# Three attention stages in another order, and latent queries in six column tiles

## The chip, the cores and the metric

The kernel runs on one core of a Trainium2 chip. The metric is device time in microseconds (us) of one launch, from runs without the profiler; one further execution was recorded by the hardware profiler, and all rows below come from it. Five engines work side by side and meet at semaphores: TensorE (PE, matrix products; PEld is its weight load), VectorE (DVE), ScalarE (ACT, with function tables), GpSimd (POOL) and SyncE (SP, which here only issues DMAs).

## The reference

256 tokens of width 1024 go through two layers of a first block and one of a second, all in float32:

```python
for l in range(DEPTH):                                   # first block, 2 layers
    a = hybrid_mixer(rms_norm(x, pre_mix_g[l]), ...)     # latent + dilated attention
    x = x + rms_norm(a, post_mix_g[l])
    c = memory_cross_attention(rms_norm(x, pre_xattn_g[l]), rms_norm(mem, mem_g[l]), ...)
    x = x + rms_norm(c, post_xattn_g[l])
    hdn = jnp.square(jax.nn.relu(rms_norm(x, pre_mlp_g[l]) @ w_up[l]))
    x = x + rms_norm(hdn @ w_down[l], post_mlp_g[l])
# second block, 1 layer
u, v, q, kv, gl = jnp.split(h @ w_in[l], splits, axis=-1)
a = spatial_gating_unit(gelu(u), gelu(v), ...)           # 128 x 128 causal mixing of tokens
b = nsa_attention(q, kv, gl, ...)                        # compressed, selected and window branches
x = x + concat(rms_norm(a, ...), rms_norm(b, ...)) @ w_out[l]
x = x + memory_cross_attention_2(...)
x = x + square(relu(h @ w_ff1[l])) @ w_ff2[l]
```

The latent queries, which the change rebuilds, are, with 8 heads of 64 plain ("nope") and 32 rotated ("rope") columns and a scale of 96 ** -0.5 in the scores:

```python
q = (rms_norm(c_q, q_norm_g) @ w_uq).reshape(B, S, 8, 96)
q = concat([q[..., :64], rope(q[..., 64:], positions)], axis=-1)
```

rope(x) is [x1 * cos - x2 * sin, x2 * cos + x1 * sin] of the two halves of 16. The compressed branch of nsa_attention joins 32 tokens to one block, sends it through gelu(flat @ w1 + b1) @ w2 + b2 and scores 15 such keys per query.

## The kernel before, in words

Every product of activations with weights is made of float32r parts. A weight chunk of 128 rows is loaded by DMA into a staging buffer (raw, 4 buffers; load_w, L164), ACT writes its rounded high part (L170, or L174 with the norm's gain), DVE the rest (L171, L175) into one of 8 whl buffers. A product is then three matmuls (mm3, L182 to L184): high by high, high by low, low by high. Activations have the same two parts in hT, oT, mem or mid, here as [2, kt, T]: all high parts of the kt chunks, then all low parts.

Three helpers run the projections over k, the chunks of 128 of the inner dimension. projA takes tokens as the PE's weights and moves 512 weight columns. projB takes weight columns as PE's weights and moves 256 tokens, by mm3 into two halves of a bank. projS does the same with two matmuls: L248 moves 512 values, the high and low tokens of chunk k, which lie 8 KB apart, and L249 moves 256. Each takes a table `at`: at[k] names a function that is called ahead of chunk k, so transposes of one stage can be put between matmuls of another. PSUM has 4 banks with the name ps, 2 with tp, and one each of pf0 and pf1.

A scheduler sets each engine's order from the order in which the code is written and from priorities: V, A and G (DVE, ACT and POOL) go through the class Ahead, whose operations count as 600 places earlier; weights use nc.vector and nc.scalar, without that. All operations through Ahead carry L135 in the profile, so there one goes by tile names.

The stages that the change touches, in order of time:

- the start: 12 small matmuls warm PE up (L469), then x is normalised and transposed. Query and key/value latents are transposed into cT by transp_split (L278) from k=2 and k=5 of the first projS; rows() (L628) transposes the rotary tables; then come key rotations (krs) and a second projS, and memory([0]) and memory([1]) transpose mem.
- latent(), once per layer: w_uq is split as 8 heads of 96 columns, L752 and L753 copy its rope columns swapped behind them (128 per head), four projB calls make q in 8 tiles of two heads, all in bank pf1, and DVE evacuates each with a multiplication by the table Mq into qT. Keys and values follow. L436 makes scores from kT and qT, L405 transposes the exponentials e, and L446 multiplies the transposes eT by the values.
- mem_attention: scores (L851) and values (L859) of two halves of 128 tokens; turn() transposes a half's queries and copies them to qT. cross2 (the second block) uses it too, with qn transposed at L1390.
- mlp: up01 makes the first two of eight column blocks; turn() transposes relu results (L902), called at k=3 of a later projection.
- mixer2: the gated part (u, v), then keys, hidden (the compressed MLP's first layer, L1083, weights cmp_w1 straight from raw), queries, and a table MIX2 that says which piece runs beside which attention group. mk and mv are projections of the second block's memory; cscores (L1273) scores the 15 compressed keys; gates() takes Exp, strips() Gelu, which lie in different function tables of ACT.

## Time and profile before

| | |
|---|---|
| Runs | 1208.45, 1209.34, 1210.66 us (median 1209.34) |
| Profiled execution | 1207.37 us |
| Span of its instructions | 1205.3 us |
| PE busy | 1178.3 us (98%) |
| PE weight loads | 981.8 us (81%) |
| DVE busy | 810.4 us (67%) |
| ACT busy | 716.5 us (59%) |
| POOL busy | 83.6 us (7%) |
| DMA | 213.12 MB, mean 177 GB/s |

The span begins with the first instruction and ends with the last; the execution holds 2.07 us more around it. A matmul counts as busy from its start to its modelled end, and the next starts before that end; so what a matmul costs in a stream is read from starts, not from its duration. "Idle before" is the time in which an engine did nothing ahead of an instruction, and the releaser is the instruction whose semaphore came last. Tile names leave buffer numbers out.

### The profile page before, as it was taken

How to read it: one execution, taken by the hardware profiler on the slowest of the kernel's cores; microseconds unless marked ns; L12 is line 12 of the kernel's file. 1: busy time of each engine (PE TensorE's matmuls, PEld its weight loads, DVE VectorE, ACT ScalarE, POOL GpSimd, SP SyncE). 2: the span in 40 equal slices, each digit the busy share in tenths (PEclk: the TensorE clock that was granted, in tenths of full speed). 3: DMA queues.
4: the chain of work that ended last, by engine and by line, in shares of the span. 5: the costliest groups of instructions: out<-in, count | busy, mean ns of one | idle time of the engine just before them, and what ended most of it. 6: DMA issues, size and time to landing. Idle time of an engine off the chain costs nothing.

```text
span 1205.3 us, 17865 instructions
## 1 busy us (share of the span) xinstructions
PE 1178.3 (98%) x6430; PEld 981.8 (81%) x6430; DVE 810.4 (67%) x1583; ACT 716.5 (59%) x1492; POOL 83.6 (7%) x161
## 2 busy tenths in 40 slices
PE   8999999999999999999999999999999999999998
PEld 6788888888888898778888788887877787888887
DVE  6777766576676676766757676667658657766653
ACT  7766655565565575755648565557676557655551
...
GB/s 263 296 183 223 98 216 196 59 233 194 191 180 197 116 265 196 148 190 157 208 90 193 240 179 200 195 178 166 198 207 106 88 88 138 211 191 188 183 192 35
DMA packets 92182, 213.12 MB, mean 177 GB/s; under 512 B 7285, under 2 KB 21055, under 8 KB 91327
## 3 DMA queue, kind: packets, MB, share of 16 engines
...
## 4 chain that ended last, share of the span: by engine, by line
PE 76%; DMA 7%; DVE 7%; ACT 6%; issue 2%; POOL 1%; SPq 0%; ACTq 0%; POOLq 0%; DVEq 0%
PE ps L184 11%; PE ps L182 11%; PE ps L183 11%; PE pf L248 8%; PE tp L248 6%; PE pf L249 4%; PE pf L182 4%; PE pf L184 4%; PE pf L183 4%; DVE whl L175 3%; PE tp L249 3%; ACT whl L174 2%; DMA raw<-in_w_in_dram 2%; PE ps L446 2%; PE ps L851 1%
## 5 line engine op out<-in xcount | busy, mean ns | idle before, releaser
L175 DVE SCALAR_TENSOR_TENSOR whl<-raw,gT,whl 128x512 fp32r<-128x512 f32 (+5 forms) x416 | 295.0, 750 | 99.1 <-ACT whl L174 98.7
L174 ACT ACTIVATE whl<-raw,gT 128x512 fp32r<-128x512 f32 (+5 forms) x416 | 277.0, 717 | 131.0 <-issue 59.8
L171 DVE TENSOR_TENSOR whl<-raw,whl 128x512 fp32r<-128x512 f32 x264 | 170.3, 686 | 79.6 <-ACT whl L170 79.1
L170 ACT ACTIVATE whl<-raw 128x512 fp32r<-128x512 f32 x264 | 153.7, 628 | 110.7 <-issue 77.7
L182 PE MATMUL ps<-whl,mid 128*128 128x512 f32 x384 | 150.5, 392 | 0.0
L184 PE MATMUL ps<-whl,mid 128*128 128x512 f32 x384 | 149.8, 390 | 0.0
L183 PE MATMUL ps<-whl,mid 128*128 128x512 f32 x384 | 149.6, 390 | 0.0
L248 PE MATMUL pf<-hT,whl 128*128 128x512 f32 x352 | 132.6, 399 | 0.0
L248 PE MATMUL tp<-hT,whl 128*128 128x512 f32 x288 | 107.9, 398 | 0.0
L249 PE MATMUL pf<-hT,whl 128*128 128x256 f32 x352 | 98.8, 281 | 0.0
L182 PE MATMUL ps<-whl,hT 128*128 128x512 f32 (+4 forms) x240 | 85.6, 356 | 0.0
L184 PEld LDWEIGHTS ps<-whl,mid 128*128 128x128 f32 x384 | 72.1, 188 | 15.6
L184 PE MATMUL ps<-whl,hT 128*128 128x512 f32 (+4 forms) x240 | 84.1, 350 | 0.4 <-DVE hT L135 0.4
L182 PEld LDWEIGHTS ps<-whl,mid 128*128 128x128 f32 x384 | 72.1, 188 | 15.1
L183 PE MATMUL ps<-whl,hT 128*128 128x512 f32 (+4 forms) x240 | 84.1, 350 | 0.0
L183 PEld LDWEIGHTS ps<-whl,mid 128*128 128x128 f32 x384 | 72.1, 188 | 14.5
L249 PE MATMUL tp<-hT,whl 128*128 128x256 f32 x288 | 80.9, 281 | 0.0
L248 PEld LDWEIGHTS pf<-hT,whl 128*128 128x128 f32 x352 | 66.1, 188 | 16.2 <-DVE qkd L135 0.3
L249 PEld LDWEIGHTS pf<-hT,whl 128*128 128x128 f32 x352 | 66.5, 189 | 0.0
L248 PEld LDWEIGHTS tp<-hT,whl 128*128 128x128 f32 x288 | 54.1, 188 | 13.2 <-DVE mem L135 0.2
L182 PE MATMUL ps<-whl,oT 128*128 128x512 f32 x152 | 60.8, 400 | 0.0
L184 PE MATMUL ps<-whl,oT 128*128 128x512 f32 x152 | 59.7, 393 | 0.0
...
## 6 DMA issues: line engine op xcount, KB each, us to landing
...
```

The lines of the kernel that those rows point to most:

```text
L170: nc.scalar.activation(hl[:, 0, c:d], raw[:, c:d], AF.Copy)
L171: nc.vector.tensor_tensor(out=hl[:, 1, c:d], in0=raw[:, c:d], in1=hl[:, 0, c:d].bitcast(F32), op=ALU.subtract)
L174: nc.scalar.activation(hi[:, i], r[:, i], AF.Copy, scale=g[i])
L175: nc.vector.scalar_tensor_tensor(lo[:, i], r[:, i], g[i], hi[:, i].bitcast(F32), ALU.mult, ALU.subtract)
L182: PE.matmul(o, sh, mh, start=start, stop=False, skip_group_check=True)
L183: PE.matmul(o, sh, ml, start=False, stop=False, skip_group_check=True)
L184: PE.matmul(o, sl, mh, start=False, stop=stop, skip_group_check=True)
L248: PE.matmul(banks[c], hi[:, cs], xT[2][:, :, k], start=k == 0, stop=False, skip_group_check=True)
L249: PE.matmul(banks[c][:, 0], lo[:, cs], xT[0][:, k], start=False, stop=k == KT - 1, skip_group_check=True)
L446: PE.matmul(cell["o"][j * 64:j * 64 + 64, h // 2], vf(h, kb), pp[j][i][kb] if bias is None else pp[j][i][kb][:, ::-1], start=begin and i = ...
L851: PE.matmul(s[:, i], qT[:, c, tq], kT[:, c], start=(i == 0 and k == 0), stop=k == nkt - 1, skip_group_check=True)
```

## The change

- latent() splits w_uq into 256 rope columns of all heads and 512 nope columns, without swapped copies. Three tiles of two times 128 columns are made, in banks pf1, pf0, pf1. The rope tile is copied by ACT to SBUF and multiplied by csq, once for cos (DVE) and once for sin (POOL), for each of four pairs of heads; the nope tiles are scaled by ACT while copied. The sum of the two products for rotation is taken over by the keys: krs holds them a second time with halves swapped.
- hT, oT and mem become [kt, 2, T]: high and low part of a chunk side by side.
- 15 warm-up matmuls. Transposes at k=1 and 6; rows() at k=2 and memory at k=5 and 7 of the second projS; krs behind it.
- turn1() ahead of values(0) in mem_attention; in cross2 the squares of the queries come from the copy qn, behind the qT copy, and the weights of the last mlp (ff1) are held until that copy.
- up01's turn at k=5, down's at n=6, mixer2's first at k=6.
- The first half of cmp_w1 is loaded ahead into a large tile (w1; oT takes its tile later), hidden(0) is spread over four places of the next projection; gates() waits for the last Gelu; ckeys and cscores stand earlier, two banks in turn.

```diff
-MIX2 = {1: "gating ckeys0 mk0 ckeys", 2: "mk1 norm0", 3: "norm1 first0 cprobs", 4: "finish0 mkn first1 rn0", 5: "mv0",
+MIX2 = {1: "gating mk0", 2: "mk1 norm0", 3: "norm1 first0 cprobs", 4: "finish0 mkn first1 rn0", 5: "mv0",
         6: "out0"}
 
 IDENT, TRI, CM, VALID, BLK, ROPE, ONES, SEL, NCOL = 0, 128, 256, 286, 288, 296, 300, 301, 331
...
-                PE.matmul(banks[c], hi[:, cs], xT[2][:, :, k], start=k == 0, stop=False, skip_group_check=True)
+                PE.matmul(banks[c], hi[:, cs], xT[2][:, k], start=k == 0, stop=False, skip_group_check=True)
...
-        h = h16p.tile([128, 2, kt, T], F32R, tag="h16", name=nm)
-        return (h[:, 0], h[:, 1], h)
+        h = h16p.tile([128, kt, 2, T], F32R, tag="h16", name=nm)
+        return (h[:, :, 0], h[:, :, 1], h)
...
-    for _ in range(12):
+    for _ in range(15):
         PE.matmul(b, warm, warm.unsqueeze(1).to_broadcast([128, 16, 32]), start=True, stop=True)
...
-        V.tensor_scalar(Mq, M, 96.0 ** -0.5, None, ALU.mult)
-        V.memset(Mq[0:64], 96.0 ** -0.5)
+        for g in range(4):
+            nc.vector.tensor_scalar(csq[32 * g:32 * g + 32, 0], M[64:96], 96.0 ** -0.5, None, ALU.mult)
+            nc.scalar.activation(csq[32 * g:32 * g + 32, 1], M[96:128], AF.Copy, scale=-(96.0 ** -0.5))
...
-                                    at={2 + 3 * t: lambda t=t: transp_split(cns[t], t, cT, 0, 5) for t in range(2)})):
+                                    at={1 + 5 * t: lambda t=t: transp_split(cns[t], t, cT, 0, 5) for t in range(2)})):
...
-            rows()
             memory = load_mem(I["mem"])
+        wd = load_all(w, 8, 1184, 512, gp)
+        for i, b in enumerate(projS(wd, hT, 4, ["ps", "ps", "pf0", "pf1"], at={2: rows, 5: lambda: memory([0]), 7: lambda: memory([1])} if l == 0 else {})):
+            halves(qkd[:, 1, i], b)
...
-                hl = whlp.tile([128, 2, 8, 128], F32R, tag="whl", name="whl")
+                hl = whlp.tile([128, 2, 768], F32R, tag="whl", name="whl")
                 g = GI["q_norm_g", l][k]
-                nc.scalar.activation(hl[:, 0, :, 0:96], raw, AF.Copy, scale=g)
-                nc.vector.scalar_tensor_tensor(hl[:, 1, :, 0:96], raw, g, hl[:, 0, :, 0:96].bitcast(F32), ALU.mult, ALU.subtract)
-                for i in range(2):
-                    f32v = hl[:, i].bitcast(F32)
-                    nc.vector.tensor_copy(hl[:, i, :, 96:112], f32v[:, :, 80:96])
-                    nc.vector.tensor_copy(hl[:, i, :, 112:128], f32v[:, :, 64:80])
-                wq.append((hl[:, 0].rearrange("p h c -> p (h c)"), hl[:, 1].rearrange("p h c -> p (h c)")))
+                for c0, n, o in ((64, 32, 0), (0, 64, 256)):
+                    hi, lo = (hl[:, i, o:o + 8 * n].rearrange("p (h c) -> p h c", h=8) for i in range(2))
+                    nc.scalar.activation(hi, raw[:, :, c0:c0 + n], AF.Copy, scale=g)
+                    nc.vector.scalar_tensor_tensor(lo, raw[:, :, c0:c0 + n], g, hi.bitcast(F32), ALU.mult, ALU.subtract)
...
-            for i in range(4):
-                b, = projB([(h_[:, i * 256:], l_[:, i * 256:]) for h_, l_ in wq], cT, 2, "pf1")
-                V.tensor_tensor(out=qT[:, 2 * i:2 * i + 2], in0=b, in1=Mq.unsqueeze(1).to_broadcast([128, 2, T]),
-                                op=ALU.mult)
+            for i in range(3):
+                b = ps([128, 2, 256], f"pf{(i + 1) % 2}")
+                for k, (h_, l_) in enumerate(wq):
+                    for c in range(2):
+                        cs = slice((2 * i + c) * 128, (2 * i + c) * 128 + 128)
+                        mm3(b[:, c], h_[:, cs], l_[:, cs], cT[0][:, k], cT[1][:, k], k == 0 and c == 0, k == 2)
+                if i == 0:
+                    rope = sc([128, 2, T])
+                    A.activation(rope, b, AF.Copy)
+                    for g in range(4):
+                        pr = slice(32 * g, 32 * g + 32)
+                        for j, eng in enumerate((V, G)):
+                            eng.tensor_tensor(out=qT[64 + 32 * j:96 + 32 * j, g:8:4], in0=rope[pr],
+                                              in1=csq[pr, j].unsqueeze(1).to_broadcast([32, 2, T]), op=ALU.mult)
+                else:
+                    h = 4 * (i - 1)
+                    for j in range(2):
+                        A.activation(qT[0:64, h + j:h + 4:2], b[64 * j:64 * j + 64], AF.Copy, scale=96.0 ** -0.5)
             for i in range(2):
                 b, = projB([(w_[0][0][:, i * 256:], w_[0][1][:, i * 256:]) for w_ in wkv], cT, 2, "pf1", k0=3)
...
+        turn1()
         values(0)
-        turn1()
...
-            ws = [load_all(w_up, 8, j * 512, 512, g) for j in range(2)]
+            if held[0] is None:
+                ws = [load_all(w_up, 8, j * 512, 512, g) for j in range(2)]
+            else:
+
+                with tc.issue_after(held[0].ins):
...
-                    at = {} if turn is None else {3: turn}
+                    at = {} if turn is None else {5: turn}
...
-            last = down(j, mids, {} if j else {3: turn})
+            last = down(j, mids, {} if j else {6: turn})
...
-            uvb = [projA(wuv[i], hT, t, [(0, 512)], at={4: first} if i == 1 and t == 0 else {})[0] for i in range(2)]
+            uvb = [projA(wuv[i], hT, t, [(0, 512)], at={6: first} if i == 1 and t == 0 else {})[0] for i in range(2)]
...
+        w1 = h16p.tile([128, 16, 256], F32, tag="h16", name="w1")
+        for q4 in range(4):
+            nc.sync.dma_start(w1[:, q4 * 4:q4 * 4 + 4],
+                              I["cmp_w1_2"][0, 0, q4 * 512:q4 * 512 + 512, :].rearrange("(m p) n -> p m n", p=128))
...
+            wib[t], = projA(ww, hT, t, [(0, 280)], at={2 * q + 1: lambda q=q: hidden(0, [q]) for q in range(4)} if t else {})
             keys(t)
-            if t == 0:
-                hidden(0)
+        oT = new_hT("oT")
...
+            with tc.issue_after(cell["gelu"].ins):
+                for t in range(2):
+                    A.activation(gate[:, t].rearrange("p h b -> p (h b)"), wib[t][:, 256:280], AF.Exp, scale=-1.0)
...
-        queries(1, projA(wq, hT, 1, [(0, 512)], "pf0", at={0: lambda: hidden(1, [2]), 2: lambda: hidden(1, [3]),
+        queries(1, projA(wq, hT, 1, [(0, 512)], "pf0", at={0: lambda: hidden(1, [2]), 1: ckeys, 2: lambda: hidden(1, [3]),
                                                            3: lambda: keysT(1), 4: lambda: queriesT(0),
-                                                           5: lambda: (strips(1), gates()), 6: gateT})[0])
+                                                           5: lambda: (strips(1), gates()), 6: gateT, 7: ckeysT})[0])
...
-            return {2 * t + h + 1: lambda t=t, h=h: some(t, h) for t in range(2) for h in range(2)}
+            return {2 * t + h + 2: lambda t=t, h=h: some(t, h) for t in range(2) for h in range(2)}
...
-               "first0": lambda: first_half(0), "first1": lambda: first_half(1), "ckeys0": ckeys0, "ckeys": ckeys,
-               "cprobs": cprobs, "finish0": lambda: cell.update(rn=finish(0)), "rn0": lambda: cell["rn"](), "mk0": lambda: mk(0), "mk1": lambda: mk(1, cscores()), "mkn": mkn,
+               "first0": lambda: first_half(0), "first1": lambda: first_half(1),
+               "cprobs": cprobs, "finish0": lambda: cell.update(rn=finish(0)), "rn0": lambda: cell["rn"](), "mk0": lambda: mk(0, cscores()), "mk1": lambda: mk(1, {1: cvalues}), "mkn": mkn,
...
-            ms = head_ms(qb, 4, 128)
-            G.tensor_tensor(out=ms[:, :4], in0=ms[:, :4], in1=r2[t][:, 1:2].to_broadcast([128, 4]), op=ALU.mult)
-            rq[t] = lv()
-            rsqrt_eps(ms[:, :4], 4, r=rq[t])
-            G.tensor_tensor(out=rq[t][:, :4], in0=rq[t][:, :4], in1=r2[t][:, 0:1].to_broadcast([128, 4]), op=ALU.mult)
-
...
-                copy_any(qT[:, :, t * 128:t * 128 + 128], bt)
+                held[0] = copy_any(qT[:, :, t * 128:t * 128 + 128], bt)
+
+                ms = head_ms(qn, 4, 128)
```

PE in cross2, between the last query projection of the second half and the output projection (L405, in the changed file L404, transposes e; L859, there L872, is eT by values; L1390, there L1414, transposes the queries; L851, there L864, makes scores). Before:

```order
L184 MATMUL pf_9443<-whl,hT 128x512
L405 MATMUL tp<-cm,e 128x128 x8
L859 MATMUL ps<-eT,kv_8921 128x128 x8
L1390 MATMUL tp<-cm,sc 128x128 x4
L851 MATMUL ps<-kv_8921,qT 128x256 x4
L182 MATMUL ps<-whl,oT 128x512
```

And of the change:

```order
L183 MATMUL pf_9421<-whl,hT 128x512
L1414 MATMUL tp<-cm,sc 128x128 x2
L404 MATMUL tp<-cm,e 128x128 x3
L1414 MATMUL tp<-cm,sc 128x128 x2
L404 MATMUL tp<-cm,e 128x128 x3
L872 MATMUL ps<-eT,kv_8899 128x128 x4
L404 MATMUL tp<-cm,e 128x128 x2
L872 MATMUL ps<-eT,kv_8899 128x128 x4
L864 MATMUL ps<-kv_8899,qT 128x256 x4
L181 MATMUL ps<-whl,oT 128x512
```

The transposes of the queries moved ahead of the value products, and they and those of e alternate. Next, ACT in mixer2, up to the exponentials of the first window scores (hc is the Gelu, small the gates, kq and vw queries and values, whl the weights of w_out). Before:

```order
L135 ACTIVATE sc<-pf_8360 128x256
L174 ACTIVATE whl<-raw,gT_99 128x1024 x2
L135 ACTIVATE scf<-pf_8360 128x512
L174 ACTIVATE whl<-raw,gT_99 128x1024
L135 ACT_TABLE_LOAD
L135 ACTIVATE e,den<-ps,sm,small 128x128 x8
L135 ACTIVATE junk,sm<-uv 128x512 x2
```

And of the change:

```order
L135 ACTIVATE hc<-hp,gT_99 128x30 x2
L135 ACT_TABLE_LOAD
L135 ACTIVATE small<-ps 128x24 x2
L135 ACTIVATE vw<-tp 128x512
L135 ACTIVATE nx<-tp,gqk 128x30
L173 ACTIVATE whl<-raw,gT_99 128x512
L135 ACTIVATE sc<-pf_8339 128x256
L173 ACTIVATE whl<-raw,gT_99 128x512
L173 ACTIVATE whl<-raw,gT_99 128x1024
L135 ACTIVATE scf<-pf_8339 128x512
L173 ACTIVATE whl<-raw,gT_99 128x1024 x2
L135 ACTIVATE e,den<-ps,sm,small 128x128 x8
L135 ACTIVATE junk,sm<-uv 128x512
```

The function table is loaded once behind the last Gelu, ahead of the gates, and one weight split more comes behind the exponentials. Last, DVE where layer 1's latent query weights are split (raw to whl). Before:

```order
L749 SCALAR_TENSOR_TENSOR whl<-raw,gT_98,whl 128x8x96
L752 CAST whl<-whl 128x8x16
L753 CAST whl<-whl 128x8x16
L752 CAST whl<-whl 128x8x16
L753 CAST whl<-whl 128x8x16
L749 SCALAR_TENSOR_TENSOR whl<-raw,gT_98,whl 128x8x96
L135 TENSOR_TENSOR scf<-pf_4768,scf 128x256
L752 CAST whl<-whl 128x8x16
L753 CAST whl<-whl 128x8x16
L752 CAST whl<-whl 128x8x16
L753 CAST whl<-whl 128x8x16
L749 SCALAR_TENSOR_TENSOR whl<-raw,gT_98,whl 128x8x96
```

And of the change:

```order
L752 SCALAR_TENSOR_TENSOR whl<-raw,gT_98,whl 128x256
L752 SCALAR_TENSOR_TENSOR whl<-raw,gT_98,whl 128x512
L752 SCALAR_TENSOR_TENSOR whl<-raw,gT_98,whl 128x256
L752 SCALAR_TENSOR_TENSOR whl<-raw,gT_98,whl 128x512
L135 TENSOR_TENSOR scf<-pf_4764,scf 128x256
L752 SCALAR_TENSOR_TENSOR whl<-raw,gT_98,whl 128x256
L752 SCALAR_TENSOR_TENSOR whl<-raw,gT_98,whl 128x512
L762 SCALAR_TENSOR_TENSOR whl<-raw,gT_98,whl 128x512 x4
```

Three splits of 8x96 with four casts each became six splits, of 256 and 512 columns, without casts.

## Rows read from the trace of the kernel before

**Rows 1.** The page: the span, and busy us of TensorE (PE).
```profile
span 1205.3 us, 17865 instructions
...
PE 1178.3 (98%) x6430; PEld 981.8 (81%) x6430; DVE 810.4 (67%) x1583; ACT 716.5 (59%) x1492; POOL 83.6 (7%) x161
```

**Rows 2.** View of PE's waits: us in total, times, longest us.
```profile
PE ps L446 <- DVE eT L135: 2.2, 2, 1.8
PE tp L902 <- DVE relu L135: 2.1, 4, 1.1
...
PE ps L859 <- ACT eT L135: 1.8, 3, 1.3
PE tp L405 <- DVE e L135: 1.7, 2, 1.6
PE tp L628 <- DVE cT L135: 1.4, 1, 1.4
PE pf L1083 <- DMA raw<-in_cmp_w_dram: 1.3, 1, 1.3
PE tp L278 <- DVE cT L135: 1.2, 1, 1.2
```

**Rows 3.** Timeline, PE, 838-844 us: start, us, operation, count, idle before.
```profile
838.39 0.85 PE L278 MATMUL tp<-cm,sc 128*128 128x128 f32 x6 [0.55 <-DVE sc L135]
...
843.04 0.50 PE L184 MATMUL ps<-whl,hT 128*128 128x512 f32 x1 [0.39 <-DVE hT L135]
```

**Rows 4.** Groups by shape, PE: operation, count, busy us, mean ns, idle before.
```profile
L182 PE MATMUL ps<-whl,mid 128*128 128x512 f32 x384 | 150.5, 392 | 0.0
...
L248 PE MATMUL pf<-hT,whl 128*128 128x512 f32 x352 | 132.6, 399 | 0.0
...
L182 PE MATMUL pf<-whl,mem 128*128 128x512 f32 x88 | 36.2, 411 | 0.2 <-ACT scf L135 0.2
...
L469 PE MATMUL pf<-mhalf 128*32 128x512 bf16 x12 | 4.8, 581 | 1.0 <-POOL mhalf L135 1.0
```

**Rows 5.** Timeline, PE, layer 0's latent queries.
```profile
116.09 0.28 PE L182 MATMUL pf<-cT,whl 128*128 128x256 f32 x1
...
117.76 0.28 PE L184 MATMUL pf<-cT,whl 128*128 128x256 f32 x1
```

**Rows 6.** Groups by shape, POOL.
```profile
L135 POOL COPY nx<-hc 128x60 f32<-128x60 f32 x4 | 1.1, 324 | 2.5 <-ACT hc L135 2.5
L135 POOL TENSOR_SCALAR_AFFINE_SELECT scf<-scf 128x1024 f32<-128x1024 f32 x1 | 1.1, 1106 | 94.9 <-DMA scf<-in_sg_w_dram 94.9
```

**Rows 7.** Timeline, PE, layer 1's latents.
```profile
518.75 1.09 PE L446 MATMUL ps<-eT,VV 128*64 128x128 f32 x16 [1.82 <-DVE eT L135]
```

**Rows 8.** Timeline, PE, cross2 and the start of its mlp.
```profile
1004.46 1.78 PE L851 MATMUL ps<-kv,qT 128*128 128x256 f32 x7 [1.30 <-ACT qT L135]
...
1021.00 0.39 PE L182 MATMUL pf<-whl,hT 128*128 128x512 f32 x1
...
1023.72 0.39 PE L182 MATMUL pf<-whl,hT 128*128 128x512 f32 x1
```

**Rows 9.** Timeline, ACT, mixer2.
```profile
899.76 1.28 ACT L135 ACT_TABLE_LOAD   x1
```

**Rows 10.** Timeline, PE, mixer2.
```profile
893.45 1.16 PE L436 MATMUL ps<-kq 64*128 64x128 f32 x16
...
914.81 1.95 PE L1273 MATMUL pf<-nx,kq 64*128 64x15 f32 x16
...
919.99 1.97 PE L446 MATMUL ps<-eT,vw 128*64 128x128 f32 x16
```

**Rows 11.** Stretches: busy PE, PEld, DVE, ACT, POOL; PEclk, DMA share, GB/s.
```profile
920.00:922.00 2.00, 2.00 (x18) 1.67 (x18) 1.90 (x8) 0.40 (x2) 0.00 (x0) 0.50 0.00 0
```

**Rows 12.** Timeline, all engines, 905.2 to 906.4 us.
```profile
905.27 1.25 DVE L175 SCALAR_TENSOR_TENSOR whl<-raw,gT,whl 128x1024 fp32r<-128x1024 f32 x1
...
905.38 1.20 POOL L135 TENSOR_TENSOR sm<-sm,epst 128x1 f32<-128x1 f32 x1 [4.88 <-ACT junk L135]
```

121 lines of the change are left out of this document (62 added, 59 removed).

## The prediction

> **What bounds the kernel now.** I read the page's head first: TensorE (PE) is busy for 1178.3 of 1205.3 us [rows 1]. So time can leave in two ways only: PE gets less to do, or its waits and slow stretches go. Next came the view of PE's waits; the seven lines that matter here are shown [rows 2]. The releasers are mostly copies on VectorE (DVE) and ScalarE (ACT) that come late for a transpose or an attention product, once a DMA; nearly all sit at stage changes, and between them PE streams. Last I read the timeline around each wait, for what stands late on the releasing engine, and the grouped instructions for prices. A wait costs a little more than its idle time, since the pipeline refills: the first 128x512 matmul behind a wait shows 0.50 us [rows 3] where the group's mean is 392 ns [rows 4], so I add 0.1 us each.
>
> The profiled execution took 1207.37 us, 2.07 more than its span; the median of the runs is 1209.34, another 1.97 above. I sum against 1207.37 and add 2.0 at the end.
>
> **The change part by part.**
>
> *Fewer query matmuls.* Per layer 24 products of three matmuls become 18, so 18 matmuls go, 36 in both layers. Fifteen of them start between 116.09 and 117.76 us, 0.119 us apart [rows 5]: 36 x 0.119 = **4.3 us**, all on PE's path. DVE loses twelve casts a layer, and its four evacuations become five ACT copies plus four multiplies each on DVE and GpSimd (POOL). No row shows a POOL multiply of 32x512. Bounds: 324 ns (128x60 copy) and 1106 ns (128x1024 select) [rows 6]; on the straight line between them 512 elements take 0.69 us, and double if two inputs cost double. The rope tile comes first; 36 nope matmuls and the first key tile (12) follow, 48 x 0.119 = 5.7 us, before scores read qT. A copy, which I put at the 0.7 us of such sizes, and four multiplies of 0.69 take 3.5; at 1.38 each they take 6.2, but the first scores need only the first. On PE 0 to 1 us, taken as 0, because the multiplies stay covered at the smaller price and the scores come head by head. The reshaped tables cost a few short instructions once, beside projections.
>
> *Layer-1 latents.* At 518.75 us PE waits 1.82 us for an eT copy on DVE [rows 7]; DVE stood behind weight splits, these behind ACT, and ACT behind a weight DMA that could start only once a staging buffer was free. Without the casts buffers come free sooner. Between 0 and 1.9; I take **1.3**, since the DMA's own time stays in that chain.
>
> *Layout.* The 512-wide operand of L248 was two runs of 256 values 8 KB apart and becomes one run. Its group shows 399 ns, L182 with mid as weights, which moves one run, 392 [rows 4]. 832 such matmuls (four groups, one shown) x 7 ns: 0 to 5.8 us. Against the full sum speaks L182 with mem as weights: it moves one run too and shows 411, so a few ns need not come from layout. I take **2**.
> The Trainium skill, page "SBUF — State Buffer", section Specifications (TRN2), says that reads lose bandwidth when they leave a 16-byte line with fewer than two hits on it. Runs of 256 values satisfy that as well as one of 512, so by it this part would be 0 and the total 2 us later; the 7 ns neither prove nor refute it.
>
> *Start stage.* The second transposes (k=5, now 6) wait 1.2 us for the copy of cT that frees their bank, and rows() 1.4 [rows 2]. A k-step there is four pairs of a 512-wide and a 256-wide matmul, 4 x (0.227 + 0.119) = 1.4 us of cover by the starts in [rows 5, 8]; rows() moves two k-steps into the next projection, 2.8 us. 2.6 idle plus refill: 1 to 2.8, I take **2.5**. Late next are the mem transposes and the qkd copies behind the second projection, small waits that stay; what the krs operations did on DVE ahead of that projection's copies comes after them now. Three more warm-up matmuls, 581 ns on the mean [rows 4], stand ahead of the first transpose on PE: 0 to 1.7 if each delays it in full, but their starts lie closer than that; I take a loss of **0.3**.
>
> *up01 and down.* Four waits of L902 for relu, 2.1 us [rows 2]. Two further k-steps are six matmuls; twelve start from 1021.00 to 1023.72 us, 0.227 apart [rows 8], so six are 1.36 us, longer than the longest wait of 1.1. 2.1 + 4 x 0.1: 1.2 to 2.6, I take **2.5**.
>
> *Cross attention.* turn1 goes ahead of values(0). L859 waits 1.8 us in three places, one of 1.3, in cross2 [rows 2]; there L851 also waits 1.30 at 1004.46 for the qT copy [rows 8]. Now transposes stand ahead of the eT products and cover part of the first wait, and the products, sixteen at no less than the 1.09 us of L446's sixteen [rows 7], cover most of the qT copy; ACT's squares move behind that copy. Cross2: 0.8 to 2.8, I take **2.0**. The two layers have the other 0.5 of L859 and as much of L851: 0 to 1, I take **0.5**, since there the turn itself may now wait. The added wait, ff1's weights behind the qT copy, queues sixteen DMAs and the splits on ACT and DVE behind it, but has 16.5 us from 1004.46 to the first matmul with them at 1021.00 [rows 8]: hidden. Without that cover a late weight would hold PE by one DMA and two splits.
>
> *mixer2, first part.* first at k=6: it waits 0.55 at 838.39 and PE again 0.39 at 843.04 for hT [rows 3]: 0 to 1.1, I take **0.8**. hidden(0) waits 1.3 for the cmp_w1 DMA [rows 2]; loaded early into a free large tile, that goes, while three more breaks of the stream come at 0.1 to 0.2: 0 to 1.4, I take **0.9**. The early load is 2 MB at the same place in SP's queue where weights follow; what is behind it there (2048, 1024) has the rest of two projections to land.
>
> *mixer2, second part.* L405 waits 1.7 for e [rows 2]; the exps stand behind a table load at 899.76 of 1.28 us [rows 9], which moves to an earlier place, and the compressed scores slide in ahead of L405 as cover: 1.9 with refill. Of these scores 16 records in one bank take 1.95, while L436, alternating row halves and banks, does 16 in 1.16 [rows 10]; two such groups, alternating now, save 0 to 1.6, I take 1.2. From 920 to 922 us the granted clock is 0.50, the level of 1.2 GHz, after PE had run those 64x15 series [rows 11]: L446 takes 1.97 there [rows 10] and 1.09 at full clock [rows 7], and its neighbours lose about as much, 1.7 together by my estimate. The series lie between 512-wide matmuls now: 0 to 1.7, I take 1.7. Waits for nx and for later eT copies, some 2.6 in lines not shown, need not go: 0 to 2.6, I take 1.2. Together **6.0**, between 0 and 7.8.
>
> Sum: 4.3+1.3+2+2.5-0.3+2.5+2.0+0.5+0.8+0.9+6.0 = 22.5. 1207.4-22.5+2.0 = 1186.9, so **1187 us**.
>
> **Rivals.**
> A. *The waits only move.* The copies and splits that end them stay in the same queues, and a PE that comes sooner stands at the next late one. For it: DVE and ACT are behind old and new waits alike. Against: most waits are short against the cover that one or two k-steps bring. Then the matmuls (4.3), half of the clock's 1.7 and a quarter of the other terms (16.5/4) remain, 9.3: **1200 us**. This is also the case in which the reordering does not do what it says.
> B. *The full layout gain*, 5.8 instead of 2: **1183 us**. For it the 7 ns, against it the 411 of mem.
> C. *POOL holds DVE up.* A POOL operation on one column lasts 1.20 us at 905.38 while DVE's split of 1.25 runs beside it [rows 12]: the two wait for each other. If DVE has to stand while POOL multiplies, eight of 0.69 us put 5.5 us on DVE, and in layer 1 PE waits for DVE as it is: 1187 + 5.5, **1192 us**. Against it: layer 0 has idle DVE time there, and in the row POOL was the one that waited.
> The Trainium skill, "SBUF — State Buffer", section Who interferes with whom, has this as an exclusive hold for a whole instruction, when DVE reads two SBUF inputs and POOL reads SBUF, with the later one blocked. The row at 905.38 agrees; for DVE as the blocked one no row speaks.
> D. *The new layout reads slower.* If hT, oT and mem come to read as mem does in L182 (411 against 392 [rows 4], 19 ns), 832 matmuls of L248 and some 1,300 with hT or oT as weights lose 2,130 x 19 ns = 40 us against the other 20.5: 1189 + 40, **1229 us**. Slower than before from 20.5/2,130 = 9.6 ns each on. Against it: where L182 moves one run of 512 with mid as weights it takes 392, and mem lies today as hT does, so its extra ns come rather from its neighbours in the stream.
>
> **How the numbers follow.** The forecast with its own range of 1177 to 1195 has 0.76, of which B holds 0.18 and C 0.1; A (1195 to 1206) 0.15; a change too small to tell 0.04; D 0.05. The poor ends of the terms sum to 4.3+1+1.2+0.8-1.7 = 5.6, the good ones to 4.3+1.9+5.8+2.8+2.6+2.8+1+1.1+1.4+7.8 = 31.5, which is 1204 and 1178 us. All poor ends at once are unlikely; a little beyond the good end lies what no row prices. The range is **1176 to 1200**. About 0.2% (2.4 us) is what a measurement of this kernel can tell from no change. Faster by more than that: 0.91; within: 0.04; slower: 0.05.
>
> **What would show it.** In the profile after: L182 to L184 with cT 36 fewer, still 0.119 us apart; no long wait of L902 for relu; none of L405 for e above 1 us; no stretch at half clock near 900 to 910 us; L851 in cross2 without its 1.3; L248 below 399 ns by what layout gave. I am wrong if the waits turn up under other names (A), if splits stretch beside POOL's multiplies (C), or if 128x512 groups grow (D).

## The result, and the profile after

The changed kernel takes 1226.69 us (median; 1224.77 to 1228.54), the kernel before took 1209.43 us on the same chip: a ratio of 1.0145, 95% interval 1.0128 to 1.0161. It is 17 us slower. I had forecast 1187 us, with 0.91 for faster and a range of 1176 to 1200, so the sign was wrong too. The span of the profiled execution grew from 1205.3 to 1225.9 us. A single launch of all those below, one of e6 at 2982 us, was far out and is left out of every number.

The head of the page after, busy time and share of the span, answers to [rows 1]:

```profile
span 1225.9 us, 17822 instructions
PE 1183.2 (97%) x6397; PEld 981.9 (80%) x6397; DVE 819.7 (67%) x1571; ACT 722.4 (59%) x1510; POOL 95.3 (8%) x169
```

PE is still busy nearly throughout. Its busy time rose by 4.9 us although it has fewer matmuls to do, a first hint of a slower clock; the other 15.7 us are waits. The view of PE's waits after, to be read against [rows 2]; columns are total, times, longest, in us:

```profile
PE pf L247 <- DVE qkd L135: 5.3, 1, 5.3
PE ps L435 <- DVE kT L135: 4.7, 2, 2.7
PE tp L277 <- DVE eT L135: 3.4, 1, 3.4
PE ps L445 <- ACT eT L135: 2.9, 2, 2.1
...
PE ps L183 <- DVE hT L135: 1.8, 1, 1.8
...
PE ps L181 <- ACT relu L135: 1.5, 1, 1.5
PE tp L404 <- DVE e L135: 1.3, 3, 0.8
...
PE tp L915 <- DVE relu L135: 1.1, 1, 1.1
```

Line numbers have shifted by a few (L182 to L184 are L181 to L183 now, L248 is L247, L278 L277, L405 L404, L436 L435, L446 L445, L859 L872, L902 L915). The waits that I had aimed at did fall: relu 2.1 to 1.1, e 1.7 to 1.3, and the one for the cT copy at L628 is gone from these rows. But five of 1.8 to 5.3 us, new or grown, stand above them, each where the change had moved a transpose or added work to DVE or ACT.

To see where the time was lost I compared the start times of the same matmul in both traces. The difference grows or shrinks, stage by stage. The first row ends where the same work has been issued in both orders: the first 128 products with mem, 24 of the first score products (L435) and eight transposes of e (L404). At the first product with mem itself the difference is only 3.3 us, but there the changed order has still to do ten score products that the old one has done.

| stage | after minus before, us | my terms there |
|---|---|---|
| start, to the end of that work | +5.6 | -2.5 + 0.3 |
| layer 0 mixer, to its output product | +1.6 | -2.2 (matmuls) |
| its output product, to cross attention | -1.4 | 0 |
| layer 0 cross attention | +2.5 | -0.25 |
| layer 0 MLP | -0.5 | -0.8 |
| layer 1 mixer, its output product | +3.8, -1.2 | -2.2, -1.3 |
| layer 1 cross attention | +2.3 | -0.25 |
| layer 1 MLP | +3.7 | -0.8 |
| mixer2, first and second part | +4.6, +1.2 | -1.7, -6.0 |
| cross2 and what lies around it | -1.0 | -2.0 |
| last MLP | -0.6 | -0.8 |
| sum | +20.6 | |

The sum is the growth of the span; the medians differ by 17.3, because the profiled execution lay 2 us below the median before and 1 us above it after. Such differences come from one trace each. The start is the same code in the changed kernel and in e2, e3, e4 and e10 below, and is +5.6 to +6.8 late there; e7, which gains and loses nothing, wanders between -0.3 and +2.3. So a single entry is good to 1 or 2 us.

My layout term of 2 us was spread over all of them. The groups of instructions by line and shape (the last two numbers are busy us and mean ns of one) show that it is nothing; they answer to [rows 4], 392 and 399 ns:

```profile
L181 PE MATMUL ps<-whl,mid 128*128 128x512 f32 x384 | 151.4, 394 | 2.1 <-ACT relu L135 1.5 <-ACT mid L135 0.6
L247 PE MATMUL pf<-hT,whl 128*128 128x512 f32 x352 | 133.9, 403 | 5.3 <-DVE qkd L135 5.3
L247 PE MATMUL tp<-hT,whl 128*128 128x512 f32 x288 | 107.9, 398 | 0.0
```

Four places lose most. **The query latents.** Their multiplies by the rope table, in the groups after:

```profile
L135 POOL TENSOR_TENSOR qT<-sc,csq 32x512 f32<-32x512 f32 x8 | 12.2, 1524 | 124.5 <-ACT sc L135 124.0
L135 DVE TENSOR_TENSOR qT<-sc,csq 32x512 f32<-32x512 f32 x8 | 10.3, 1286 | 0.3 <-ACT sc L135 0.2
```

I had taken 0.69 us for one on POOL, from [rows 6]. Both engines show about twice that. The timeline after (start, duration) shows DVE and POOL in layer 0, then DVE and PE in layer 1:

```profile
121.07 5.76 DVE L135 TENSOR_TENSOR qT<-sc,csq 32x512 f32<-32x512 f32 x4 [0.19 <-ACT sc L135]
121.17 6.82 POOL L135 TENSOR_TENSOR qT<-sc,csq 32x512 f32<-32x512 f32 x4 [60.81 <-ACT sc L135]
126.86 2.34 DVE L174 SCALAR_TENSOR_TENSOR whl<-raw,gT,whl 128x512 fp32r<-128x512 f32 x2
526.75 1.57 DVE L135 TENSOR_TENSOR qT<-sc,csq 32x512 f32<-32x512 f32 x1
528.36 2.61 DVE L135 TENSOR_SCALAR e<-e,den 128x256 f32<-128x256 f32 x2
532.75 0.62 DVE L135 TENSOR_SCALAR e<-e,den 128x256 f32<-128x256 f32 x2
539.88 1.37 PE L435 MATMUL ps<-kT,qT 128*128 128x128 f32 x6 [2.66 <-DVE kT L135]
```

In layer 0, one by one (the timeline of narrower windows shows them apart):

```profile
121.07 0.69 DVE L135 TENSOR_TENSOR qT<-sc,csq 32x512 f32<-32x512 f32 x1 [0.19 <-ACT sc L135]
121.79 1.67 DVE L135 TENSOR_TENSOR qT<-sc,csq 32x512 f32<-32x512 f32 x1
122.98 1.63 POOL L135 TENSOR_TENSOR qT<-sc,csq 32x512 f32<-32x512 f32 x1
126.86 1.68 DVE L174 SCALAR_TENSOR_TENSOR whl<-raw,gT,whl 128x512 fp32r<-128x512 f32 x1
128.46 0.74 DVE L174 SCALAR_TENSOR_TENSOR whl<-raw,gT,whl 128x512 fp32r<-128x512 f32 x1
```

The first multiply on DVE takes 0.69 us, the later ones 1.67; the split that follows takes 1.68 while POOL's last multiply runs, the one behind it 0.74. Beside POOL the two e operations at 528.36 take 2.61 us; at 532.75, without it, 0.62. The splits at 126.86 take 2.34 together, where two take 1.41 elsewhere. Everything behind them on DVE is late, in the end the kT copies for which L435 waits.

**The start.** ACT, DVE and PE ahead of the second projection:

```profile
49.04 0.72 ACT L173 ACTIVATE whl<-raw,gT 128x512 fp32r<-128x512 f32 x1 [2.21 <-DMA raw<-in_w_in_dram]
49.79 1.69 ACT L623 ACTIVATE csq<-scf 32x256 f32<-32x256 f32 x4
54.72 0.75 ACT L135 ACTIVATE cT<-tp 128x512 fp32r<-128x512 f32 x2
57.35 0.88 DVE L135 TENSOR_TENSOR cT<-tp,cT 128x512 fp32r<-128x512 f32 x2
58.15 0.74 DVE L135 TENSOR_TENSOR qkd<-pf,qkd 128x256 f32<-128x256 f32 x2
58.61 0.79 PE L247 MATMUL pf<-hT,whl 128*128 128x512 f32 x1 [5.30 <-DVE qkd L135]
```

The second cT transposes now stand just ahead of the end of the projection, so the cT copies and the qkd copies of that end come together on both engines, DVE's behind a normalisation and a split. ACT reaches its cT copies only at 54.72, behind the four table operations (csq), three splits and the squares of a norm. PE stands for 5.30 us.

**The MLP of layer 1.** The copies that follow the moved relu transposes, on ACT and PE:

```profile
683.85 0.72 ACT L173 ACTIVATE whl<-raw,gT 128x512 fp32r<-128x512 f32 x1 [1.49 <-DMA raw<-in_w_up_dram]
684.48 0.58 ACT L135 ACTIVATE mid<-tp 128x512 fp32r<-128x512 f32 x1
685.11 0.50 PE L181 MATMUL ps<-whl,mid 128*128 128x512 f32 x1 [0.63 <-ACT mid L135]
687.97 0.79 PE L181 MATMUL ps<-whl,mid 128*128 128x512 f32 x1 [1.46 <-ACT relu L135]
```

The mid copy stands behind a split that waits 1.49 us for a weight DMA. With two k-steps more ahead of the transposes there are two fewer behind them to cover that.

**mixer2.** Its first part, where first moved from k=4 to k=6, and its second part:

```profile
859.24 0.75 DVE L135 SCALAR_TENSOR_TENSOR uv<-uv,sm,gb 128x512 f32<-128x512 f32 x1 [1.75 <-POOL sm L135]
860.63 1.28 DVE L135 TENSOR_TENSOR hT<-tp,hT 128x512 fp32r<-128x512 f32 x2
861.37 0.51 PE L183 MATMUL ps<-whl,hT 128*128 128x512 f32 x1 [1.79 <-DVE hT L135]
936.37 1.34 ACT L173 ACTIVATE whl<-raw,gT 128x512 fp32r<-128x512 f32 x2 [1.84 <-DMA raw<-in_w_mkv_dram]
938.18 0.69 DVE L135 COPY eT<-tp 128x512 f32<-128x512 f32 x1
939.01 0.63 PE L277 MATMUL tp<-cm,sc 128*128 128x128 f32 x4 [3.35 <-DVE eT L135]
941.76 1.98 PE L445 MATMUL ps<-eT,vw 128*64 128x128 f32 x16 [2.12 <-ACT eT L135]
```

The transposes at k=6 leave two k-steps, six matmuls, of cover for the hT copies, and DVE makes its copies behind a layer norm of uv that waits 1.75 us for POOL. Around 939 the eT copies stand behind the compressed scores' arithmetic on DVE and behind splits that wait for a DMA on ACT. The stretches by window of that place (busy us of PE, PEld, DVE, ACT, POOL, then the granted clock, DMA share, GB/s):

```profile
941.00:943.00 2.00, 1.24 (x12) 1.24 (x14) 2.00 (x10) 2.00 (x9) 0.00 (x0) 0.50 0.71 240
943.00:945.00 2.00, 2.00 (x14) 1.17 (x12) 1.32 (x5) 1.57 (x6) 0.27 (x2) 0.50 0.59 225
945.00:947.00 2.00, 2.00 (x12) 1.26 (x9) 0.68 (x2) 0.00 (x0) 0.94 (x1) 0.50 0.00 0
947.00:949.00 2.00, 2.00 (x13) 1.74 (x12) 2.00 (x7) 0.60 (x3) 0.00 (x0) 0.99 0.00 0
```

The half clock of [rows 11] did not go. It moved, and lasts 6 us here where it lasted about 3 before. It also appears behind the long wait of the start (0.53, 0.50 and 0.67 from 56 to 64 us), behind the stops of layer 1's MLP (0.62 from 688 to 692), behind layer 1's wait for kT (0.72 and 0.50 from 540 to 544) and behind the wait for hT (0.68 and 0.50 from 861 to 865).

### The profile page after: what moved, and what is told of

It is laid out like the page before. It is cut to its first block, busy times and chain, and to the rows that moved or that the text cites. A ratio compares the mean times of both kernels' runs of the same rounds, so it can differ in the third digit from the quotient of the medians.

```text
span 1225.9 us, 17822 instructions
## 1 busy us (share of the span) xinstructions
PE 1183.2 (97%) x6397; PEld 981.9 (80%) x6397; DVE 819.7 (67%) x1571; ACT 722.4 (59%) x1510; POOL 95.3 (8%) x169
## 4 chain that ended last, share of the span: by engine, by line
PE 79%; DVE 6%; ACT 4%; DMA 3%; issue 2%; POOL 1%; SPq 0%; ACTq 0%; DVEq 0%; POOLq 0%
PE ps L181 12%; PE ps L183 12%; PE ps L182 12%; PE pf L247 8%; PE tp L247 6%; PE pf L248 4%; PE pf L181 4%; PE pf L183 3%; PE pf L182 3%; PE tp L248 3%; DVE whl L174 2%; PE ps L435 2%; PE ps L445 2%; PE ps L864 1%; PE tp L404 1%
## 5 line engine op out<-in xcount | busy, mean ns | idle before, releaser
L181 PE MATMUL ps<-whl,mid 128*128 128x512 f32 x384 | 151.4, 394 | 2.1 <-ACT relu L135 1.5
L183 PE MATMUL ps<-whl,mid 128*128 128x512 f32 x384 | 150.4, 392 | 0.2 <-DVE mid L135 0.2
L182 PE MATMUL ps<-whl,mid 128*128 128x512 f32 x384 | 150.1, 391 | 0.0
L247 PE MATMUL pf<-hT,whl 128*128 128x512 f32 x352 | 133.9, 403 | 5.3 <-DVE qkd L135 5.3
L247 PE MATMUL tp<-hT,whl 128*128 128x512 f32 x288 | 107.9, 398 | 0.0
L248 PE MATMUL pf<-hT,whl 128*128 128x256 f32 x352 | 99.4, 282 | 0.0
L181 PE MATMUL ps<-whl,hT 128*128 128x512 f32 (+4 forms) x240 | 86.7, 361 | 0.4 <-ACT hT L135 0.4
L181 PEld LDWEIGHTS ps<-whl,mid 128*128 128x128 f32 x384 | 72.5, 189 | 17.9 <-ACT relu L135 1.8
L183 PE MATMUL ps<-whl,hT 128*128 128x512 f32 (+4 forms) x240 | 84.6, 353 | 1.8 <-DVE hT L135 1.8
L183 PEld LDWEIGHTS ps<-whl,mid 128*128 128x128 f32 x384 | 72.4, 188 | 16.3 <-DVE mid L135 0.6
L182 PE MATMUL ps<-whl,hT 128*128 128x512 f32 (+4 forms) x240 | 84.8, 353 | 0.0
L247 PEld LDWEIGHTS pf<-hT,whl 128*128 128x128 f32 x352 | 66.7, 189 | 22.0 <-DVE qkd L135 5.9
L182 PEld LDWEIGHTS ps<-whl,mid 128*128 128x128 f32 x384 | 72.6, 189 | 14.5
L248 PE MATMUL tp<-hT,whl 128*128 128x256 f32 x288 | 80.9, 281 | 0.0
L248 PEld LDWEIGHTS pf<-hT,whl 128*128 128x128 f32 x352 | 67.1, 191 | 0.0
L247 PEld LDWEIGHTS tp<-hT,whl 128*128 128x128 f32 x288 | 54.1, 188 | 13.2 <-DVE mem L135 0.2
L181 PE MATMUL ps<-whl,oT 128*128 128x512 f32 x152 | 60.8, 400 | 0.0
L182 PE MATMUL ps<-whl,oT 128*128 128x512 f32 x152 | 59.5, 391 | 0.0
```

The costliest lines, as they stand in the source:

```text
L181: PE.matmul(o, sh, mh, start=start, stop=False, skip_group_check=True)
L182: PE.matmul(o, sh, ml, start=False, stop=False, skip_group_check=True)
L183: PE.matmul(o, sl, mh, start=False, stop=stop, skip_group_check=True)
L247: PE.matmul(banks[c], hi[:, cs], xT[2][:, k], start=k == 0, stop=False, skip_group_check=True)
L248: PE.matmul(banks[c][:, 0], lo[:, cs], xT[0][:, k], start=False, stop=k == KT - 1, skip_group_check=True)
```

## The experiments

The totals below are medians with the ratio to the kernel before, measured beside each; a "mark" is the difference of the same matmul's start to the kernel before, from the table's points. (The recorded texts of e13 to e17 take the mark of the start at the last mem transposes, and name +3.0 for the changed kernel and +2.1 for e11; these are +5.6 and +2.6 here.)

**e1: the start in its old order, the rest changed.**

```
- at={1 + 5 * t: ...transp_split...}    + at={2 + 3 * t: ...}
- at={2: rows, 5: memory 0, 7: memory 1}  + rows(), krs first, then at={6: memory 0}
```

> The changed kernel with the start stage in the old order (transposes at k=2 and 5, rows() and the mem load between the two projections, memory at 6 and behind, key rotations ahead). Theory, late copies: the wait of L247 for qkd at 58.6 us (5.3) and the half clock behind it (about 1.7) go, and the old waits of 1.2 and 1.4 come back: 4 to 6 us less than the changed kernel, about 1221. Rival, the new layout or the table copies on ACT slow the start whatever the order: under 1 us less, about 1226.

1223.74 us, 1.0111 (1.0082 to 1.0141); the interval overlaps the changed kernel's. Mark of the start +1.8 instead of +5.6. So in the trace the moved transposes are some 3.7 us of the start's loss, and not the whole of it.

**e2: all rope multiplies on DVE.**

```
- for j, eng in enumerate((V, G)):
+ for j, eng in enumerate((V, V)):
```

> The changed kernel with all eight multiplies of the rope tile on VectorE, none on GpSimd. Theory, the two engines shut each other out: VectorE's mean falls from 1286 ns to about 0.7 us, so eight hold it for about 5.6 us, as long as four do now, and the time stays within 1.5 us of the changed kernel (1225 to 1228). Rival, a 32x512 multiply simply takes VectorE 1.29 us: eight hold it for 10.3 us, and kT is late by 4.5 us more in each layer: about 1235.

1220.76 us, 1.0089 (1.0063 to 1.0116), clear of the changed kernel's interval. Its group:

```profile
L135 DVE TENSOR_TENSOR qT<-sc,csq 32x512 f32<-32x512 f32 x16 | 11.0, 685 | 0.5 <-ACT sc L135 0.2
```

Sixteen multiplies take DVE 11.0 us alone; eight beside POOL took 10.3. So POOL's eight bought DVE 0.7 us, and held up whatever DVE did next. The wait for kT, 4.7 us, is not among the ten largest any more, and in the marks the two mixers lose 4.5 us less. The gain was larger than either theory had said.

**e3: relu transposes back at k=3.**

```
- else {5: turn}   ...  {6: turn}
+ else {3: turn}   ...  {3: turn}
```

> The changed kernel with the relu transposes of up01 and down back at k=3 and n=3. Theory, moving them later took away the cover of the copy behind them: in layer 1 the four waits around 680 to 688 us and the slow clock behind them go, 3.7 us less there, while 0.5 us each comes back in layer 0 and in the last mlp: 2 to 3.5 us less, about 1224. Rival, the weights' DMA is what is late there: no gain, 1226 to 1228.

1225.85 us, 1.0129 (1.0105 to 1.0153): no clear gain. In the trace layer 1's MLP loses 1.8 us instead of 3.7, the last mark is +19.5. So about half of that loss goes with the moved transposes. The other half stays in the old order; ACT stands for a weight DMA there too (2.56 us), which may be its cause but was not tested.

**e4: mixer2 as before, the rest changed** (the old function whole, with its table of pieces).

```
- MIX2 = {1: "gating mk0", ...              (new mixer2)
+ MIX2 = {1: "gating ckeys0 mk0 ckeys", ... (old mixer2)
```

> The changed kernel with mixer2 wholly in the old order (first at k=4, hidden(0) in one piece, gates, ckeys and cscores where they were). Theory: the waits of 1.8 us for hT, of 3.4 and 2.1 us for eT and the slow clock from 941 to 947 us go, the old waits come back: 3 to 6 us less than the changed kernel, about 1222. Rival: the wait for eT comes from work that is late from earlier stages, and stays: under 1 us.

1222.07 us, 1.0106 (1.0068 to 1.0143). In the trace mixer2 goes from +5.8 to -2.0, a gain of 7.7 us; the medians show 4.6, with a wide interval that overlaps the changed kernel's. In the traces it holds the largest single loss. PE's wait of 3.35 is gone, and the granted clock is 1.00 from 919 to 930 us.

**e5: the latents and tables alone, the rest as before.**

```
- Mq, 4 groups of two column tiles, one DVE multiply each
+ csq, 6 column tiles, pf0/pf1 in turn, 4 multiplies on V and 4 on G
```

> The kernel before with the latent queries of the change alone (six column tiles, two banks, multiplies on VectorE and GpSimd, tables in the new shape), all else in the old order and layout. Theory, the engines shut each other out: each multiply takes twice its time, the 5.8 us in which VectorE does nothing else make kT late, and the 4.3 us of matmuls that go are given back: within 2 us of before, more likely 0 to 4 above (1209 to 1213). Rival, the latents pay and the order alone costs: about 1205.

1216.88 us, 1.0048 (1.0033 to 1.0064). What removes 36 matmuls is slower with its tables than the kernel before (this edit also drops an instruction at the start, see e15). Marks: start +4.9 already, then layer 0's mixer +1.9 and layer 1's +4.8.

**e6: e5 with the multiplies reading the bank, POOL out of it.**

```
- rope copied by ACT; eight 32x512 multiplies, four on V, four on G
+ rope[:, j] = b * csq[:, j]: two 128x512 multiplies on V; then eight 32x512 copies, A and V
```

> As the run with the latents alone, but the rope tile is multiplied straight from PSUM by two 128x512 operations on VectorE, and eight copies of 32x512 (four on ScalarE, four on VectorE) bring it into qT; GpSimd does nothing here. Theory: VectorE is held for about 3.5 us in small pieces instead of 5.8, kT comes in time, and the gain of the matmuls appears: 3 to 5 us below before, about 1205. Rival: ScalarE's eight copies now hold its queue, and nothing is gained: 1208 to 1211.

1211.06 us, 0.9999 (0.9983 to 1.0014). From the start's +3.8 the marks now fall to +2.8 at the end: without POOL the latents gain, but the start still costs 3.8.

**e7: the layout alone.**

```
- xT[2][:, :, k]   [128, 2, kt, T]
+ xT[2][:, k]      [128, kt, 2, T]
```

> The kernel before with hT, oT and mem as chunk by chunk pairs of high and low part, and nothing else. Theory of the prediction: 0 to 5.8 us less, 2 taken, about 1207. From the trace of the changed kernel, where L247 still shows 398 to 403 ns: no change, 1208.5 to 1210.5. Rival D: 20 us more.

1211.02 us, 1.0004 (0.9991 to 1.0017). The layout does nothing, either way.

**e8: a chosen version.** e6's latents, the layout, turn1 first in cross2 alone, the later relu transposes in layer 0 and the last MLP, all else as before.

```
+ if cover is None: values(0); turn1()
+ else:             turn1(); values(0)
+ {3 if extra else 5: turn}  ...  {3 if extra else 6: turn}
```

> The changed kernel with the parts kept that did not cost in its trace: the fixed latents, the new layout, cross2 with the turn first, the later relu transposes in layer 0 and in the last mlp; start stage, cross attention of the layers, layer 1's mlp and mixer2 in the old order. If the losses of the other parts are independent of these: 4.3 us of matmuls, 0.9 in cross2 and 1 in the two mlps, about 1203. If every gain is taken back by the queue behind it: 1207 to 1210.

1206.29 us, 0.9973 (0.9957 to 0.999): faster than both. In the layers, where the turn is old, cross attention costs 0 in the marks instead of +2.5 and +2.3; in cross2 the new order keeps 0.8.

**e9: the changed kernel with two table operations at once, six copies later.**

```
+ V.tensor_scalar(csq[64:96, 0], M[64:96], ...); V.tensor_scalar(csq[96:128, 1], M[96:128], ...)
+ (behind the second projection) tensor_copy / activation to the other partitions, x6
```

> The changed kernel with the rotary tables made in two short operations on VectorE where eight on VectorE and ScalarE stood, and six copies that fill the table up behind the second projection. Theory, the four table operations on ScalarE (1.69 us) stand ahead of the copies that free the transposes' bank and the projections' banks, and PE's long wait of 5.3 us then also costs the clock: the wait at 58.6 us shrinks below 3 us, no half clock behind it, 2.5 to 4 us less than the changed kernel, about 1223. Rival, the order of the transposes alone makes the copies late: the wait stays above 4 us.

1226.1 us, 1.0133 (1.0116 to 1.015): nothing. The copies still ran on ACT at 51.19 us, ahead of the same work: the scheduler takes what is ready, not what is written later. So it tested nothing about the tables.

**e10: first back at k=4 in mixer2.**

```
- at={6: first}
+ at={4: first}
```

> The changed kernel with first in mixer2 back at k=4. Theory, at k=6 only two chunks are left before the next projection reads the hT that these transposes make: the wait of 1.8 us for hT and that of 0.4 go, 0.55 comes back: 1.5 to 2.5 us less by the end of that projection. Rival: the copies are late because of the layer norm in front of them on VectorE, and the wait stays.

1223.96 us, 1.0123 (1.0105 to 1.0141). The interval overlaps the changed kernel's. In the trace mixer2's first part loses 2.5 instead of 4.6: k=6 cost 2.1 us where I had booked a gain of 0.8.

**e11 and e12: e8 with e9's tables and shorter copies; then with the changed start order.**

```
+ qT's nope columns by ACT and V; rope copies behind them      (e11, e12)
+ at={1 + 5 * t: ...}, rows and memory inside the projection   (e12)
```

> The chosen parts again, with the late tables and the nope tiles copied by two engines ahead of the rope's copies. Against the earlier chosen run (1206.3): 2.5 to 3 us less in the start, where the wait of 3.4 us for cT and the half clock go, and 1 to 2 in the latents, where PE waits for ScalarE's copies: about 1202. Rival, both are taken back by the next copy: 1206.

> As the run before it in this list, but with the start stage in the order of the change (transposes at k=1 and 6, rows() and memory inside the second projection). If that order pays as forecast once the tables are out of the way: 1 to 2.5 us less than that run, about 1200. If the copies of the later transposes hold the second projection's banks by themselves: 1 to 3 us more.

e11: 1205.55 us, 0.9971 (0.9958 to 0.9983). e12: 1208.16 us, 0.9985 (0.9972 to 0.9998). So e11 comes out at its rival. The start's mark is +2.6 and +7.2: the changed order costs 4.6 us there in the traces, where I had booked a gain of 2.5. The medians show 2.6, with intervals that overlap; the profiled execution of e12, 1211.41 us, was the slowest of its ten.

What remained open was the start: late by 1.8 to 7.2 us in every version with the new tables, the old order included.

**e13 and e14: no table is made in the start** (the changed kernel, and e11).

```
+ M = csq[:, 0]
+ (in latent(), l == 0) two tensor_scalar and six copies, from M
```

> The changed kernel, with the rope tables made nowhere in the start stage: the sine table M stays where csq lies, and the two scalings and six copies run inside layer 0's latents, just ahead of the query products. Theory (table work in the start stage makes ScalarE and VectorE late for the mem squares, the cT copies and the qkd copies): the copies for the second transposes and for the first wait of the next projection come earlier, the start stage comes 2 to 4 us earlier than in the changed kernel (stage mark at the last mem transposes at +0 to +1 us against before instead of +3.04), and the total falls to 1222 to 1225 us. If layer 0's latents pay for the same work instead, the mark of layer 0's mixer end stays near +6.9 and the total near 1226. Rival (the new order of the projections and of the memory loads alone makes the start late): the mark stays at +3 and the wait of about 5.5 us of the query and key matmuls for qkd stays.

> The chosen version of e11 (start stage in the old order, rope multiplied by two wide VectorE operations, old mixer2, cross2 alone turning first), with the tables made inside layer 0's latents. Theory: the start stage loses its 2 to 3 us of lateness (mark at the last mem transposes +0 to +0.5 instead of +2.08), the wait for cT falls from 2.6 to about 1.4 us, and the total comes to 1202 to 1205 us, ratio 0.994 to 0.997. Rival (the order in which the input weights are loaded, not the tables, is what is late): mark still at +2, total as e11, 1205.6.

e13: 1224.99 us, 1.0128 (1.0112 to 1.0144), mark +6.2. e14: 1205.38 us, 0.996 (0.9942 to 0.9979), mark +3.4. Neither is told apart from the version that it was made from. The tables' copies still went to ACT at 51.93 us in e14, so moving them by the program's text fails again. But in both the order differs from that of before long before any table exists, and in the same way as in the changed kernel. ACT near 23 us, in the kernel before and then in the changed one:

```profile
23.05 1.39 ACT L174 ACTIVATE whl<-raw,gT 128x288 fp32r<-128x288 f32 x3 [1.09 <-PE pf L184]
24.61 0.49 ACT L135 ACTIVATE junk<-ps 128x384 bf16<-128x384 f32 x1 [0.17 <-PE ps L184]
```

```profile
23.43 0.49 ACT L135 ACTIVATE junk<-ps 128x384 bf16<-128x384 f32 x1 [2.04 <-PE ps L183]
23.91 0.53 ACT L173 ACTIVATE whl<-raw,gT 128x288 fp32r<-128x288 f32 x1
```

After, the squares of a projection's output stand ahead of weight splits that need not wait for it, and ACT stands idle for 2.04 us. What the change takes from the program so early is one instruction: the row of ones, in the timeline of the kernel before

```profile
0.88 0.20 POOL L135 MEMSET ones<- 1x128 f32 x1
```

**e15, e16, e17: that memset alone.** e15 is the kernel before without it; e16 the changed kernel and e17 the chosen e11 with it.

```
- G.memset(ones1, 1.0)          (e15; ones1 set later, inside ktab)
+ G.memset(ktab[0:1], 1.0)      (e16, e17; overwritten later)
```

> The kernel before with one thing changed: the row of ones (a one-partition memset on GpSimd at the very start) has no tile of its own and is set later in mixer2 inside ktab, and b2 takes a slice of Mq; no tables, no latents, no moved transposes. Theory (the compiler-side scheduler orders the start stage anew when this memset is gone: the splits, the load of the positions and the weight loads change places): the mark at the last mem transposes comes 2 to 3 us late and the total is 1211 to 1213 us. Rival (the tables on ScalarE and VectorE make the start late): mark within 0.5 us of before, total 1209 to 1210.5 us.

> The changed kernel with the memset put back at its place on GpSimd (writing ktab, which is overwritten later). Theory: the first 60 rows of each queue return to the order of before up to the moved transposes; the mark at the last mem transposes falls from +3.0 to between 0 and +2, the total from 1226 to 1223 to 1225 us. Rival (tables, or the moved transposes alone): mark stays near +3, total 1226.

> The chosen version of e11 with that memset put back in the same way and nothing else changed. Theory: start as in the kernel before but for the tables, mark at the last mem transposes 0 to +0.7 us instead of +2.08, the wait for cT 1.4 instead of 2.4 us, total 1202 to 1204 us, ratio about 0.995. Rival: mark still near +2, total 1205.5 us as e11.

e15: mark +2.6; 1212.09 us, 1.0011 (0.9997 to 1.0025), so its total is not told from no change, but its start is that of the late versions. e16: mark +2.4 instead of +5.6; 1223.17 us, 1.0108 (1.0092 to 1.0124), clear of the changed kernel's interval. e17: mark +1.0 instead of +2.6; 1202.96 us, 0.9943 (0.993 to 0.9956), the fastest of all. In the traces of e16 and e17 the three splits stand ahead of the squares again, as in the kernel before; in e15 they stand behind. The head of e17's page:

```profile
span 1201.7 us, 17813 instructions
PE 1173.2 (98%) x6394; PEld 978.2 (81%) x6394; DVE 813.1 (68%) x1580; ACT 725.9 (60%) x1513; POOL 87.3 (7%) x162
```

The longest of PE's waits in it, and ACT's timeline ahead of it:

```profile
PE tp L925 <- DVE relu L135: 3.8, 2, 2.9
```

```profile
657.07 0.63 ACT L135 ACTIVATE junk<-sc 128x512 bf16<-128x512 f32 x1 [2.37 <-DMA sc<-in_mem_dram]
```

A memset of 0.20 us orders the start stage anew, and takes or gives 1.5 to 3 us of the mark. Why the scheduler's plan turns on it, I have not found; each of the three edits also moves a small tile (ktab or b2), which was not told apart from the instruction. e17 comes to layer 1's MLP 3.5 us early and loses 2.5 of them there in the wait shown: ACT stands 2.37 us for a load of mem, its splits behind. That is rival A at work in a faster kernel.

## Why the prediction was wrong

**Query matmuls: the step "on PE 0 to 1 us, taken as 0" failed.** The 4.3 us for 36 matmuls look right in size: with POOL out of the way and the start mended (e17), the two mixers with their output products gain 1.6 and 2.3 us of the marks, 3.9 together, in which the matmuls are not told apart from the rest of the new latents. But the multiplies do not run side by side: they take turns. A multiply on DVE that takes 0.69 us alone takes 1.67 beside POOL, a split 1.68 instead of 0.74, an e operation 1.27 instead of 0.35 (the first of the two at 528.36). Each time DVE stands for about 0.95 us, which is my estimate for one multiply on POOL, where I had put 0.69. Three multiplies and a split in layer 0, two multiplies and two e operations in layer 1 stand like that, some 7.7 us by the same estimate. This is rival C, which I gave 0.1 and priced at 5.5 us, eight times 0.69; undoing it (e2) gives 5.9 by the medians. That the two come so close is luck: e2 takes 7.7 us of standing off DVE and puts eight multiplies, 5.5 us, on it, and what PE gains does not follow from DVE's time alone. My odds were wrong, and the poor end of 1 us that I gave this step is missing from my sum of the poor ends. I held that the one row with both engines, [rows 12], showed POOL waiting and not DVE; I let one row with the other order decide.

The Trainium skill, "SBUF — State Buffer", section Who interferes with whom, says that the shared port pair is held for a whole instruction and that issue order, not the kind of operation, decides who is blocked. The trace agrees, for DVE as the blocked one (the split of 1.68 us, else 0.74; 2.61 us for two e operations, else 0.62).

**Moved transposes: I priced the wait ahead of them and not the copy behind them.** This step failed four times, with the same form. In the start I booked 2.5 us and the order costs 2.6 by the medians, whose intervals overlap (e12 against e11), and 3.7 and 4.6 in the traces (the changed kernel against e1, e12 against e11). For first at k=6 I booked 0.8 and it costs 2.1 (e10). For relu in up01 and down I booked 2.5: layer 0 and the last MLP gained 0.5 and 0.6, layer 1, where the copies stand behind splits that wait for a weight DMA, lost 3.7, about half of it by the order (e3). In the layers' cross attention I booked 0.5 and turn1 first costs about 2.4 each (e8 has 0 with the old order); cross2, booked at 2.0, gained 0.8 to 1.0. A k-step of cover put in front of a transpose is taken from behind it, and there it hid the copy into hT, mid, cT or eT. I wrote of the two layers' turn that it "may now wait", and never asked it elsewhere.

**mixer2, second part: the 6.0 failed.** The chain from scores to w_out loses 1.2 instead, with its first part 5.8; e4 puts the price of the new function at 7.7 in the trace. L405's wait for e did shrink from 1.6 to 0.8. But the compressed scores that were to cover it put their arithmetic on DVE ahead of the eT copies, so PE waits 3.35 and 2.12 behind, and the half clock that I had booked as gone (1.7) follows these waits.

**The start: a step that I did not have.** I read the order of the moved transposes, not the issue order from its first row. Beside that order, the memset that went made the start late: putting it back takes 3.1 us off the changed kernel's mark and 3.5 off its median (e16), leaving it out alone makes the kernel before 2.6 us late in the mark (e15). The two overlap, since together they come to more than the 5.6. The tables "beside projections" are not needed for this: e15 has none of them, e16 has all. What they cost by themselves no run shows. With the memset in place e16, in the changed order, is 1.4 us later in the mark than e17, in the old one (they differ in warm-ups and tables too), so what the order costs depends on the plan that it meets. A rival of this size stood nowhere in my list.

**Layout.** Nothing instead of 2.0 (e7), so B and D fall with it. The 0 that followed from the Trainium skill, "SBUF — State Buffer", section Specifications (TRN2), agrees with e7's ratio of 1.0004.

**Layer-1 latents.** Their 1.3 cannot be seen apart: in the changed kernel the multiplies swallowed it.

The forecast as a whole counted the cover that a move brings and not the cover that it takes. A and C were both true, and I had weighed each as if the others did not happen. My poor ends came to 1204 and the range ended at 1200, because for every moved transpose the poor end was 0 or a gain, never a loss.
